# Rolling the columns of a matrix: unaligned long pieces and direct wrapped ends in place of a staged head

## The chip, the cores and the metric

The kernel runs on one core of a Trainium2 chip. The metric is the device time of the program in microseconds, the median of several runs. A core has 16 DMA engines, which move all data here, and several instruction engines which issue the DMAs: SP and ACT, each with a hardware queue (a ring) of its own, and POOL with a software queue. HBM is the chip's main memory, in which the input and output lie; SBUF is the core's on-chip memory of 128 partitions.

## The reference

The whole computation is a rotation of every row by 100 columns.

```python
def setup_inputs():
    return {
        "x": np.random.randn(8192, 8192).astype(np.float32),
        "shift": 100,
    }

def reference(x, shift):
    return np.roll(x, shift, axis=1)
```

A row has 8192 floats, or 32,768 bytes. Output columns 100 to 8191 are input columns 0 to 8091 of the same row, and output columns 0 to 99 (400 bytes, the wrapped end) are input columns 8092 to 8191. No value is changed, so the kernel is a copy of 268.44 MB whose pieces lie 400 bytes further on in the output than in the input.

## The kernel before

With `s = 100` the kernel sets `a = 256`: `s` is rounded up to a multiple of 128 columns, and one more 128 is added where that stays small. The output is cut at column 256, which is byte 1024 of a row.

The body, columns 256 to 8191, goes from HBM to HBM by the loop that ends at L43. The rows are taken in 128 blocks of 64. In the view `(c e j) w -> c j e w` the block is `c`, `e` is one of 16 and `j` one of 4, so that the DMA for one `j` has 16 rows, each four rows from the next, and each of the 16 DMA engines gets one row piece of 31,744 bytes. Even `j` are issued on SP and odd `j` on ACT. In the last 4 blocks each row is cut in two halves, so there are 264 DMAs per queue. A DMA on SP or ACT waits, by the semaphores that the framework gives out, for the fourth DMA before it on its own queue: four are in flight per queue.

The head, columns 0 to 255, goes through SBUF on POOL's queue. It consists of the wrapped end (columns 0 to 99) and of columns 100 to 255. The rows are split into four groups `k` of 2048, each with 128 partitions, `J = 4` and `Q = 4`. For three of every four rows (`q` from 1) a contiguous run of 256 floats is read that starts 100 columns before the row (L73), so it holds the end of the row before and the beginning of this row. The wrapped end of the fourth row and the beginning of the first are read by themselves (L74, L77), and two VectorE copies (L75, L78) put the pieces of each row together in the tile `h`. Then 16 DMAs write `h` to the output, 1024 bytes per row (L82). Nothing else waits for this work, and the body does not wait for it.

Of the kernel before, what the change touches and what calls it, by code (L numbers as in the profile page):

```python
# [1 line left out]

# [4 lines left out]


@with_exitstack
def kernel(  # L10
    ctx: ExitStack,
    tc: tile.TileContext,
    x: bass.AP,
    shift: int,
    out: bass.AP,
):
    nc = tc.nc
    n_rows, n_cols = x.shape
    s = shift % n_cols
    a = -(-s // 128) * 128  # L20
    if 0 < a <= 384 and a + 128 <= n_cols:
        a += 128
    g = a - s
    P = nc.NUM_PARTITIONS
    engines = [nc.sync, nc.scalar]
    n_chunks = 16
    rows = n_rows // n_chunks

    xm = x.rearrange("(c e j) w -> c j e w", e=16, j=4)
    om = out.rearrange("(c e j) w -> c j e w", e=16, j=4)
    if a < n_cols:
        blocks = n_rows // 64
        mid = (a + n_cols) // 256 * 128
        for c in range(blocks):
            parts = ((a, mid), (mid, n_cols)) if c >= blocks - 4 and a < mid else ((a, n_cols),)  # L40
            for j in range(4):
                for lo, hi in parts:
                    engines[j % 2].dma_start(out=om[c, j, :, lo:hi], in_=xm[c, j, :, lo - s:hi - s])  # L43
    if a == 0:
        return


    if a > 512:
        for i in range(n_chunks):
            r = slice(i * rows, (i + 1) * rows)  # L50
            nc.gpsimd.dma_start(out=out[r, :s], in_=x[r, n_cols - s:])
            if g > 0:
                nc.gpsimd.dma_start(out=out[r, s:a], in_=x[r, :g])
        return

    Q, J = 4, 4  # L60
    n_st = n_rows // (P * Q * J)
    reads = ctx.enter_context(tc.tile_pool(name="reads", bufs=n_st))
    heads = ctx.enter_context(tc.tile_pool(name="heads", bufs=n_st))
    xt = x.rearrange("(k p j q) c -> k q p j c", q=Q, j=J, p=P)
    ot = out.rearrange("(k p j q) c -> k q p j c", q=Q, j=J, p=P)
    tiles = []
    for k in range(n_st):
        t = reads.tile([P, Q - 1, J, a], x.dtype)
        h = heads.tile([P, Q, J, a], x.dtype)
        for q in range(1, Q):  # L70
            lead = bass.AP(tensor=x.tensor, offset=(k * P * J * Q + q) * n_cols - s,
                           ap=[[J * Q * n_cols, P], [Q * n_cols, J], [1, a]])
            nc.gpsimd.dma_start(out=t[:, q - 1], in_=lead)  # L73
        nc.gpsimd.dma_start(out=h[:, Q - 1, :, :s], in_=xt[k, Q - 1, :, :, n_cols - s:])  # L74
        nc.vector.tensor_copy(h[:, :Q - 1, :, :s], t[:, :, :, :s])  # L75
        if g > 0:
            nc.gpsimd.dma_start(out=h[:, 0, :, s:], in_=xt[k, 0, :, :, :g])  # L77
            nc.vector.tensor_copy(h[:, 1:, :, s:], t[:, :, :, s:])  # L78
        tiles.append(h)
    for k, h in enumerate(tiles):  # L80
        for q in range(Q):
            nc.gpsimd.dma_start(out=ot[k, q, :, :, :a], in_=h[:, q])  # L82


# [1 line left out]
_INS = ['x', 'shift']  # L86
_OUTS = [((8192, 8192), 'float32')]

_NUMBERS = {'shift': 100}


# [26 lines left out]
```

## Time and profile before

| What | Before |
|---|---|
| Median time, 3 runs | 829.27 us (829.12 to 830.45) |
| Span of the profiled execution | 817.9 us |
| VectorE busy | 7.7 us |
| POOL busy | 28.9 us |
| Body DMAs: SP and ACT, 248 each of 496 KB, 16 each of 248 KB | 12.7 us and under 6 us from issue to landing |
| Head writes: 16 of 512 KB | 112.6 us from issue to landing |

In a profile page, a slice is a fortieth of the span. The row "DMA" gives the mean busy share of the 16 DMA engines in tenths, and "GB/s" what they moved, each byte counted once per DMA. A queue's line gives its packets, its bytes in MB and the time that its packets took, as a share of 16 engines' span. q1 and q10 are the two hardware rings; q0 is POOL's. The HBM line adds up what was read from HBM and what was written to it, so a byte copied from HBM to HBM counts in both. In a table of stages, each line is a stretch of the span with the engines' busy times, the clock, the DMA share and the GB/s.

### The profile page before, as it was taken

Reading aid. Unit: us, or ns where it says so; the run is one execution under the profiler, and the core shown is the slowest. Engines: PE = TensorE matmul, PEld = TensorE weight load, DVE = VectorE, ACT = ScalarE, POOL = GpSimd, SP = SyncE. Lnnn points to the kernel's source line nnn. Section 1 sums busy time; section 2 is a strip of 40 time slices with the busy share of each in tenths; the row PEclk is TensorE's granted clock in tenths of the full one; section 3 lists DMA queues with packets and bytes.
Section 4 is the critical chain, followed back from the end, with each engine's and each line's share of the span. In section 5 each row is a group of like instructions: output and inputs, shape, how many; then the busy total and the mean of one; then the engine's idle time right before and its main releaser. Section 6 shows DMA issues by size and latency. Waiting matters only on the chain. (4 is left out here: it accounts for less than half of the span.)

```text
span 817.9 us, 633 instructions
## 1 busy us (share of the span) xinstructions
DVE 7.7 (1%) x8; POOL 28.9 (4%) x40
## 2 busy tenths in 40 slices
DVE  0000000000000000000000000000000000000000
POOL 3000000010010000000000000000000000000000
DMA  9999999999999999999999999999999999999998
GB/s 307 333 348 342 347 355 347 355 356 344 350 338 363 359 351 354 361 346 360 334 333 341 326 335 331 331 332 337 328 338 331 330 336 331 335 334 326 331 308 299
DMA packets 21572, 276.89 MB, mean 339 GB/s; under 512 B 9024, under 2 KB 9024, under 8 KB 13120
## 3 DMA queue, kind: packets, MB, share of 16 engines
q10 hardware_dynamic: 8448, 130.04, 46.5%
q1 hardware_dynamic: 8448, 130.04, 45.9%
q0 software_dynamic: 4672, 16.78, 6.9%
q14 instruction: 4, 0.03, 0.0%
HBM read 268.44 MB, written 268.44 MB: 656 GB/s over the span
## 5 line engine op out<-in xcount | busy, mean ns | idle before, releaser
L82 POOL DMA_DIRECT2D out_dram<-h x16 | 13.2, 827 | 196.6 <-DMA out_dram<-h 112.1
L73 POOL DMA_DIRECT2D t<-in_x_dram x12 | 9.5, 795 | 60.4 <-DMA h<-in_x_dram 30.1
L75 DVE COPY h<-t 128x1200 f32<-128x1200 f32 x4 | 3.1, 785 | 233.6 <-DMA t<-in_x_dram 233.6
L78 DVE COPY h<-t 128x1872 f32<-128x1872 f32 x4 | 4.9, 1224 | 0.0
L74 POOL DMA_DIRECT2D h<-in_x_dram x4 | 3.0, 749 | 45.6 <-DMA t<-in_x_dram 45.6
L77 POOL DMA_DIRECT2D h<-in_x_dram x4 | 3.0, 751 | 42.8 <-DMA t<-in_x_dram 42.8
L99 POOL MEMSET const-float32-0.0<- 128x1 f32 x1 | 0.1, 100 | 0.2 <-issue 0.2
L99 POOL MEMSET const-bfloat16-1.0<- 128x1 bf16 x1 | 0.1, 103 | 0.0
L99 POOL MEMSET const-float32-1.0<- 128x1 f32 x1 | 0.1, 100 | 0.0
L99 POOL MEMSET const-uint8-127<- 128x1 uint8 x1 | 0.1, 100 | 0.0
## 6 DMA issues: line engine op xcount, KB each, us to landing
out_dram<-in_x_dram ACTq DMA_DIRECT2D x248, 496.0 KB, 12.7
out_dram<-in_x_dram SPq DMA_DIRECT2D x248, 496.0 KB, 12.7
out_dram<-h POOLq DMA_DIRECT2D x16, 512.0 KB, 112.6
t<-in_x_dram POOLq DMA_DIRECT2D x12, 512.0 KB, 95.4
out_dram<-in_x_dram SPq DMA_DIRECT2D x16, 248.0 KB, 5.7
out_dram<-in_x_dram ACTq DMA_DIRECT2D x16, 248.0 KB, 5.9
h<-in_x_dram POOLq DMA_DIRECT2D x4, 312.0 KB, 92.0
h<-in_x_dram POOLq DMA_DIRECT2D x4, 200.0 KB, 97.9
```

The lines of the kernel that those rows point to most:

```text
L73: nc.gpsimd.dma_start(out=t[:, q - 1], in_=lead)
L74: nc.gpsimd.dma_start(out=h[:, Q - 1, :, :s], in_=xt[k, Q - 1, :, :, n_cols - s:])
L75: nc.vector.tensor_copy(h[:, :Q - 1, :, :s], t[:, :, :, :s])
L77: nc.gpsimd.dma_start(out=h[:, 0, :, s:], in_=xt[k, 0, :, :, :g])
L78: nc.vector.tensor_copy(h[:, 1:, :, s:], t[:, :, :, s:])
L82: nc.gpsimd.dma_start(out=ot[k, q, :, :, :a], in_=h[:, q])
L99: nc = _bacc.Bacc("TRN2", target_bir_lowering=False, num_devices=1)
```

## The change

The change drops the cut at column 256, the whole trip through SBUF, POOL's queue and the VectorE copies. Everything goes from HBM to HBM on the two rings.

- The long piece of a row now starts at output column 100. It is 8092 columns, or 32,368 bytes, read from the beginning of the input row and written at byte 400 of the output row.
- A DMA has 32 rows: in the view `(c e h t) w -> c t e h w` each of the 16 engines gets two rows (`h`) which lie two rows apart. SP has `t = 0`, ACT has `t = 1`. The rows of a block thus stand in the same order on each ring as before. There are 128 such DMAs per queue, and no rows are halved at the end.
- The wrapped ends of a block's 64 rows, 400 bytes each, are one DMA, four pieces per engine, issued on ACT and SP in turn. There are 64 such DMAs per queue.

Its purpose is to move each byte by one DMA only, without staging.

```diff
     s = shift % n_cols
-    a = -(-s // 128) * 128
-    if 0 < a <= 384 and a + 128 <= n_cols:
-        a += 128
...
     engines = [nc.sync, nc.scalar]
...
-    xm = x.rearrange("(c e j) w -> c j e w", e=16, j=4)
-    om = out.rearrange("(c e j) w -> c j e w", e=16, j=4)
-    if a < n_cols:
-        blocks = n_rows // 64
-        mid = (a + n_cols) // 256 * 128
-        for c in range(blocks):
-            parts = ((a, mid), (mid, n_cols)) if c >= blocks - 4 and a < mid else ((a, n_cols),)
-            for j in range(4):
-                for lo, hi in parts:
-                    engines[j % 2].dma_start(out=om[c, j, :, lo:hi], in_=xm[c, j, :, lo - s:hi - s])
...
-        for q in range(1, Q):
-            lead = bass.AP(tensor=x.tensor, offset=(k * P * J * Q + q) * n_cols - s,
-                           ap=[[J * Q * n_cols, P], [Q * n_cols, J], [1, a]])
-            nc.gpsimd.dma_start(out=t[:, q - 1], in_=lead)
-        nc.gpsimd.dma_start(out=h[:, Q - 1, :, :s], in_=xt[k, Q - 1, :, :, n_cols - s:])
-        nc.vector.tensor_copy(h[:, :Q - 1, :, :s], t[:, :, :, :s])
...
-    for k, h in enumerate(tiles):
-        for q in range(Q):
-            nc.gpsimd.dma_start(out=ot[k, q, :, :, :a], in_=h[:, q])
+    xb = x.rearrange("(c e h t) w -> c t e h w", e=16, h=2, t=2)
+    ob = out.rearrange("(c e h t) w -> c t e h w", e=16, h=2, t=2)
+    xw = x.rearrange("(c e j) w -> c e j w", e=16, j=4)
+    ow = out.rearrange("(c e j) w -> c e j w", e=16, j=4)
+    for c in range(n_rows // 64):
+        for t in range(2):
+            engines[t].dma_start(out=ob[c, t, :, :, s:], in_=xb[c, t, :, :, :n_cols - s])
+        if s > 0:
+            engines[1 - c % 2].dma_start(out=ow[c, :, :, :s], in_=xw[c, :, :, n_cols - s:])
```

## The prediction

> **What bounds the kernel now.** I read the page first: slices, packets, queues and the HBM line.
>
> ```profile
> DMA  9999999999999999999999999999999999999998
> GB/s 307 333 348 342 347 355 347 355 356 344 350 338 363 359 351 354 361 346 360 334 333 341 326 335 331 331 332 337 328 338 331 330 336 331 335 334 326 331 308 299
> DMA packets 21572, 276.89 MB, mean 339 GB/s; under 512 B 9024, under 2 KB 9024, under 8 KB 13120
> ...
> q10 hardware_dynamic: 8448, 130.04, 46.5%
> q1 hardware_dynamic: 8448, 130.04, 45.9%
> q0 software_dynamic: 4672, 16.78, 6.9%
> ...
> HBM read 268.44 MB, written 268.44 MB: 656 GB/s over the span
> ```
>
> The queue shares add to 99.3%: the 16 DMA engines have a packet in hand almost all the time. That does not yet say that the engines are the limit, since a packet waiting for memory also counts as busy. The slices show about 350 GB/s while the POOL queue runs (slices 3 to 20) and about 332 after it, so I asked for stages.
>
> ```profile
> core 0: us, DVE busy (x) POOL busy (x), PEclk, DMA share, GB/s
> ...
> 180.00:345.00 165.00, 3.28 (x4) 11.10 (x13) 1.00 1.00 353
> 345.00:500.00 155.00, 0.00 (x0) 2.14 (x3) 1.00 1.00 339
> ```
>
> and, of the stages where only the two rings work, and of the edges:
>
> ```profile
> 780.00:800.00 20.00, 0.00 (x0) 0.00 (x0) 1.00 0.89 299
> 800.00:817.90 17.90, 0.00 (x0) 0.00 (x0) 1.00 0.84 297
> ...
> 0.00:4.00 4.00, 0.00 (x0) 2.91 (x8) 1.00 0.44 135
> ...
> 540.00:780.00 240.00, 0.00 (x0) 0.00 (x0) 1.00 1.00 333
> ```
>
> A byte on a ring crosses HBM twice (read and write), one on the POOL queue once, because its other end is SBUF. From 540 to 780 us HBM moves 2 x 333 = 666 GB/s. Cutting the packet records of the trace into 20 us steps and counting ring bytes twice and POOL bytes once gives 645 to 662 GB/s from 40 to 240 us and 650 to 676 after. The sum over HBM stays put while the DMA rate changes, so the bound is HBM traffic.
>
> The packet records agree. A row piece of 31,744 B takes 1.174 us at best (27.0 GB/s; 2,121 of 7,936 are under 1.2 us), but 1.467 us in the mean and about 1.515 in the ring-only stage. While POOL packets keep 2 to 3 of the 16 engines, the other 13 to 14 run at 22 to 24 GB/s each; alone, 16 run at 20.7. Fewer engines on the rings run faster each: they share something, and have slack.
>
> **What the Trainium skill says.** "HBM Reference", Specifications (TRN2), gives about 716 GB/s per domain; the 666 here is 93% of it, so the trace agrees that HBM is near. "DMA: Bandwidth & Descriptors", Issuing engines are not separate DMA queues: all issuers share the same 16 engines; the shares that add to 99.3% agree. The same page, Specifications: under 512 B a DMA does a read-modify-write. The trace has no HBM write under 1,024 B, so no run here shows it; its 400 B reads into SBUF are no slower at best (4,400 B in 171 ns, 25.7 GB/s). The same page, How a descriptor splits into AXI transactions: transactions start at 256 B boundaries, so an unaligned start costs a partial first one. The body now reads from byte 624 of a row, which is unaligned, and still reaches 27.0 GB/s. The section is illustrated by reads; writes are not seen here.
>
> **The change, part by part.** HBM traffic: before, each byte of x is read once and each of out written once. After, the same: 536.87 MB. What leaves is the SBUF trip of columns 0 to 255, so DMA bytes fall from 276.89 to 268.44 MB (3%), q0 with its 6.9% of engine time (0.069 x 817.9 = 56 us per engine) ends, and DVE (7.7 us) and POOL (28.9 us) fall idle. Under an HBM bound these were hidden beside the rings and are worth nothing of themselves.
>
> Body: the ring's pieces grow from 31,744 to 32,368 B, 8,192 of them, at the ring-only rate. Whole output at that rate: 268.44 MB / 333 GB/s = 806.1 us. This includes the bytes of the wraps.
>
> Start: 4 us at 135 in place of 333 GB/s loses 4 x (1 - 135/333) = 2.4 us. It stays.
>
> End: before loses 20 x 34/333 + 17.9 x 36/333 = 4.0 us. It coincides with the half-row pieces of the last 4 blocks: a queue's DMA waits for the fourth before it on that queue, so with half pieces half as much is in flight, and the share falls to 0.89 and 0.84. After, rows stay whole, but an engine gets two rows per DMA, so the last engine may end a row or two (1.5 us each) late. I take 3 us (2 to 5).
>
> Waits: in the built program each DMA of SP or ACT still waits for the fourth before it on its queue. Behind a waiting one stand only that queue's later DMAs, and the DMA engines wait for them once they have drained. Of three DMAs one is a wrap, so four in flight hold at least two long ones: 2 x 2 = 4 rows per engine and ring, where now there are 4 x 1. When the oldest waits for its slowest engine, the others still have up to 4 rows rather than 3. I cost it at nothing; the rows in flight hide it. Issue: 192 instructions per queue, now 264 at 0.51 us (135 us of 818). Even at 1 us each, 192 us, they would lie beside the transfers.
>
> Wraps: 8,192 pieces of 400 B, 512 per engine, in 128 groups of four. Lower bound, by the nearest row (4,096 B packets, 0.158 us at best, four pieces each): 128 x 0.158 = 20 us of engine time. Upper bound, by the slow tail of the 4,000 B packets made of 400 B pieces (0.99 us at the 95th percentile): 128 x 0.99 = 127 us. Slack to hide it: 512 rows x (1.515 - 1.174) = 175 us per engine. As bytes the wraps are already counted; for broken memory words at the seam I add two extra 64 B reads per row (my assumption), 8,192 x 128 B = 1.05 MB / 666 GB/s = 1.6 us, and round it down to 1 with the smaller number of completions. So the small value is taken on the path, and the large one opens the range.
>
> Sum: 806.1 + 2.4 + 3 + 1 = 812.5 us of span, against 817.9. The timed median is 829.27 - 817.9 = 11.4 us above the span; kept, it gives 823.9, say 824.
>
> **Rivals.**
> Wraps on the path: an HBM-to-HBM piece of 400 B may hold its engine. At 0.99 us a group, 127 us or 16% of engine time is in small packets, much as in the POOL stages, where HBM ran near 655 instead of 666: 1.7% of 806, or +14, gives 838. At 2 us a group, 256 us, the rows' 512 x 1.174 x 1.02 = 613 us no longer fit beside them: 869 of span, 880 in time. The read-modify-write note speaks for it; the undisturbed 400 B reads and the 175 us slack speak against. I put it at 838, from 829 to 872.
>
> Unaligned writes broken all along the row: column 100 is byte 400, 16 bytes past a 64 B word. If every write of 256 B broke two words rather than only a row's first and last, HBM would read another 128 B per 256 B: 536.87 + 134 = 671 MB, 1,007 us of span, 1,020 or so. For: the trace shows only aligned HBM writes. Against: the unaligned reads of today show no extra traffic; had they needed 64 B more per 256 B, the stage would move 666 x 1.125 = 749 GB/s, over the stated 716.
>
> Engines as the bound: then dropped engine time is a gain. 512 rows x 1.467 x 32,368/31,744 = 766, wraps 20, completions 128 x 3 x 9 ns = 3.5, edges 5.4: 795 of span, 806 in time. Against it stands that ring packets slow to 1.515 us when the POOL packets go.
>
> **How the numbers follow.** HBM bound with cheap wraps 0.52 (816 to 830; 0.46 faster, 0.05 same, 0.01 slower); wraps on the path 0.26 (0.04 same, 0.22 slower); broken writes 0.14, slower; engines the bound 0.08, faster. So faster 0.54, same 0.09, slower 0.37. The likeliest gives 824. The range from 807 to 872 leaves out the broken writes (0.14) and about half of the engine case.
>
> **What would show it.** Right: HBM line near 660 GB/s over the span, slices level near 333 GB/s with no step at 400 us, long packets at a mean near 1.54 us with a floor near 1.20, wrap packets well under 0.25 us for four pieces, no half-row dip at the end. Wrong: the floor of the long packets above 1.20 us or their mean above 1.6 at equal bytes (broken writes); wrap packets of 0.5 us and more, or a DMA share below 0.97 in mid-span (wraps or waits on the path); slices above 340 (engines had been the bound).

## The result and the profile after

The changed kernel takes 839.06 us (837.30 to 843.37, 6 runs) against 829.35 us for the kernel before on the same chip: a ratio of 1.0114, with a 95% interval of 1.0089 to 1.0138. A repetition gave 1.0132 (1.0111 to 1.0152). The forecast was 824 us and "faster". It is slower by 1.1 to 1.3%.

One thing must be put right before the profiles are compared. The chips differ by about 1%: the kernel before has a median of 819.7 us on one chip of the runs below, and of 827.9 to 828.4 us on the three others. The profile of before that the prediction read has a span of 817.9 us. In every run whose span and time are both known, the time is 1.7 to 2.2 us above the span. That profile thus shows an execution of about 820 us, not one of 829, most likely one on a quicker chip. So all comparisons below are ratios to the kernel before on the same chip, and profiles are set beside others of like speed.

The page of the profile after has these lines of DMA: slices, packets, queues, HBM.

```profile
DMA  9999999999999999999999999999999999999996
GB/s 300 323 331 328 317 338 318 327 325 321 324 322 326 308 326 317 328 323 319 323 316 324 317 322 323 316 310 324 321 326 310 325 319 320 317 328 319 331 331 218
DMA packets 22530, 268.48 MB, mean 319 GB/s; under 512 B 14336, under 2 KB 14336, under 8 KB 14336
q1 hardware_dynamic: 11264, 134.23, 50.1%
q10 hardware_dynamic: 11264, 134.23, 48.4%
HBM read 268.44 MB, written 268.44 MB: 638 GB/s over the span
```

The POOL queue is gone, HBM moves the same 536.87 MB, and the step at 400 us is gone, all as foreseen. But the level rate is about 320 GB/s and not 333, and the last slice falls to 218. The stages of the same run, with the same columns as before:

```profile
core 0: us, POOL busy (x), PEclk, DMA share, GB/s
0.00:4.00 4.00, 0.20 (x4) 1.00 0.51 170
...
540.00:780.00 240.00, 0.00 (x0) 1.00 0.99 320
...
820.00:841.40 21.40, 0.00 (x0) 1.00 0.66 224
```

In the ring-only stage HBM now moves 2 x 320 = 640 GB/s, and in the last 21 us a third of the engines' time is empty, that is, no packet is in hand. The packet records show that the wraps are not slow themselves: a 400 B packet takes 22 to 24 ns at the median and 29 ns in the mean, 0.12 us for a group of four. The long packets have their floor at 1.199 us, which is the floor of before scaled to their length (1.174 x 1.02 = 1.197). Their mean is 1.584 us, where 1.54 was foreseen. So neither kind of packet is slow in its own engine at its quickest; what has fallen is the rate that the engines reach together.

### The profile page after: what moved, and what is told of

The parts are those of the page before. It is cut to its first block, busy times and chain, and to the rows that moved or that the text cites. A ratio compares the mean times of both kernels' runs of the same rounds, so it can differ in the third digit from the quotient of the medians.

```text
span 841.4 us, 429 instructions
## 1 busy us (share of the span) xinstructions
POOL 0.2 (0%) x4
## 3 DMA queue, kind: packets, MB, share of 16 engines
HBM read 268.44 MB, written 268.44 MB: 638 GB/s over the span
```

## Experiments

**The same two kernels on equally quick chips.** First the kernel before, unchanged.

> The kernel before, unchanged, profiled on the same chip as the next three. In the profile of the change the time is 2.0 us above the span (843.37 against 841.4), where the prediction put 11.4 us. If the 11.4 us belong to the kernel before (its POOL queue), the span here is again about 818 with a time near 829. If they are only a profile taken of a quicker execution, the span here is the time less 2 us, about 827, and the HBM sum of the ring-only stage is then below 666 GB/s.

It took 828.52 us (1.0004, 0.9992 to 1.0017), with a span of 827.2 us. Its queues and stages:

```profile
q1 hardware_dynamic: 8448, 130.04, 46.3%
q10 hardware_dynamic: 8448, 130.04, 46.3%
q0 software_dynamic: 4672, 16.78, 6.9%
```

```profile
20.00:400.00 380.00, 7.70 (x8) 22.59 (x28) 1.00 1.00 346
400.00:780.00 380.00, 0.00 (x0) 0.00 (x0) 1.00 1.00 329
```

So on a chip where this kernel takes 828 us, its ring-only stage runs at 329 GB/s, not 333, and the 11.4 us above the span do not exist. The two errors cancelled in the sum: 268.44 MB / 329 is 816 us plus 2, where the prediction had 806 plus 11.4. They are not what turned the sign.

The changed kernel was repeated where before took 828.08 us.

> The changed kernel, unchanged, profiled on the same chip as the next three. Time near 838, span 2 us less, about 320 to 322 GB/s in the middle, and an end of about 10 us in which 4 to 8 engines still work.

It took 838.99 us, with a span of 834.4 us in the profiled execution. The queue lines of its page, and its stages:

```profile
q1 hardware_dynamic: 11264, 134.23, 49.9%
q10 hardware_dynamic: 11264, 134.23, 48.7%
```

```profile
0.00:10.00 10.00, 0.20 (x4) 1.00 0.84 300
20.00:780.00 760.00, 0.00 (x0) 1.00 0.99 324
804.40:834.40 30.00, 0.00 (x0) 1.00 0.78 266
```

The shares give an account of engine time. Here they add to 98.6%, with 12.2 us of the span empty by the packet records; in the kernel before they add to 99.5%, with 4.7 us empty. Packets fill 822.2 us here and 822.5 us there. So dropping 56 us of POOL packets per engine left the filled time where it was, and 7.5 us of emptiness were added: the changed kernel has 3.8 us of it in mid-span and 5.7 us in the last 30 us, where before has none and 3.2. These are single executions; the changed one is 2.5 us quicker than the median of its kernel. The rest of the study asks what refilled the 822 us, and where the emptiness comes from.

**Long pieces without wraps.** Two twins write 8064 columns per row and no wrapped end.

```diff
-            engines[t].dma_start(out=ob[c, t, :, :, s:], in_=xb[c, t, :, :, :n_cols - s])
-        if s > 0:
-            engines[1 - c % 2].dma_start(out=ow[c, :, :, :s], in_=xw[c, :, :, n_cols - s:])
+            engines[t].dma_start(out=ob[c, t, :, :, 100:8164], in_=xb[c, t, :, :, 0:8064])     # unaligned
+            engines[t].dma_start(out=ob[c, t, :, :, 128:8192], in_=xb[c, t, :, :, 28:8092])    # aligned
```

> Left out: the wrapped ends and the last 28 columns; 8064 columns per row are written from column 100 (source column 0), two rows per engine and DMA as in the change. 264.24 MB, which at the 320.5 GB/s of the changed kernel's steady stretch takes 824.5 us, plus about 7 us for start, end and launch: 832. Theory A (the unaligned writes slow HBM): 828 to 834, and slower by 15 us or more than the aligned twin. Theory B (the 400 B wraps slow HBM, or break up the long pieces): the rate returns to about 333 GB/s and the time to about 802, like the twin.

> Left out: output columns 0 to 127. The same 8064 columns per row, but written from column 128 (byte 512) and read from column 28 (byte 112): write aligned, read not. Theory A: long packets at the floor and mean of the kernel before, 333 GB/s, 793 + 9 = 802 us. Theory B: the same time as the unaligned twin, 802. Theory C (two rows per DMA slow the steady rate, nothing else): both near 830.

The ratios are 0.9824 (0.9793 to 0.9855) and 0.9805 (0.9781 to 0.9830): 814.64 and 812.78 us. Both twins run their level stages at 327 to 329 GB/s, close to before's ring-only stage; both have this same line:

```profile
400.00:780.00 380.00, 0.00 (x0) 1.00 1.00 328
```

A row that is written from an unaligned start is therefore not broken all along: the rival of 1,020 us is refuted, and so is any large price on the long pieces. From the unaligned twin to the changed kernel lie, by the ratios (1.0114 and 1.0132), 24 to 26 us for 4.19 MB, which by bytes would be 13. The wraps, or what they meet, cost 11 to 13 us above their bytes.

**What makes a wrap dear.** Three kernels change the size of the wrap, in the changed kernel's layout. Two of them do a rotation by another amount (`roll128`, `roll200`), and the third writes four columns less.

```diff
-            engines[t].dma_start(out=ob[c, t, :, :, s:], in_=xb[c, t, :, :, :n_cols - s])
+            engines[t].dma_start(out=ob[c, t, :, :, 128:], in_=xb[c, t, :, :, :n_cols - 128])  # or 200
-            engines[1 - c % 2].dma_start(out=ow[c, :, :, :s], in_=xw[c, :, :, n_cols - s:])
+            engines[1 - c % 2].dma_start(out=ow[c, :, :, :128], in_=xw[c, :, :, n_cols - 128:])  # or 200
+            engines[1 - c % 2].dma_start(out=ow[c, :, :, :96], in_=xw[c, :, :, n_cols - 100:n_cols - 4])  # ends96
```

> Other work: a rotation by 128 columns. The same bytes and the same DMAs, but long pieces of 32,256 B written at byte 512 and wraps of 512 B, all starts aligned. Theory S (8,192 wraps under 512 B, or words broken at the seam, make HBM read again): both causes are gone, and the steady rate returns to the 328 GB/s of the long pieces alone: 814 us plus 4.2 MB / 328 GB/s x ... as bytes, 12.8, so 826 to 828. Theory P (the price is per piece, a fixed cost of each of the 8,192 small packets): the wraps still cost about as much over their bytes, 836 to 839.

> Other work: a rotation by 200 columns. Wraps of 800 B, over 512 B, but neither 800 nor its half is a multiple of 64 B, so words at the seam stay broken. If wraps under 512 B are dear because they are under 512 B: 826 to 829. If broken words at the seam cost: as the changed kernel, 837 to 840. Theory P (per piece): also 837 to 840, since the pieces are as many.

> Left out: output columns 96 to 99. Wraps of 384 B, a multiple of 64, so that wraps break no word; the long pieces still start in the middle of one, as in the changed kernel. If the wraps' own partial words cost: 829 to 833. If it is their size under 512 B, or their number: 838, less 0.1 MB of bytes (0.4 us).

The rotation by 128 took 0.9950 of before (0.9938 to 0.9962), the one by 200 took 0.9980 (0.9966 to 0.9993), and the wraps of 384 B took 1.0035 (1.0023 to 1.0047), all beside the repeated changed kernel at 1.0132. So a fixed price per piece falls: all have 8,192 wraps, and two of them beat the kernel before. Cutting the wrap from 400 to 384 B saved 0.97%, 8 us, with 0.05% fewer bytes. The rotation by 200 was meant to keep broken words of 64 B above a size of 512 B, and it was cheap; but 800 B is a multiple of 32, so two readings were left, a limit at 512 B and a word of 32 B. The next three kernels part them.

> Other work: a rotation by 104 columns. Wraps of 416 B, a multiple of 32 but not of 64, still under 512; long pieces start at byte 416. Theory T32 (what costs is a broken word of 32 B): the price of the changed kernel goes, 824 to 830. Theory T64 (a broken word of 64 B): 836 to 839 as the changed kernel. Theory N (under 512 B as such costs): as the run with wraps of 384 B, about 830, and not lower.

> Other work: a rotation by 196 columns. Wraps of 784 B, over 512 B, that break a word of 32 B in its middle as the 400 B wraps do; the run with 800 B did not. If the broken word costs whatever the size of the piece: 835 to 839. If it costs only in pieces under 512 B: as the rotation by 200 columns, 825 to 828.

> Left out: output columns 100 to 103. Wraps of 400 B as in the changed kernel, but the long pieces are written from column 104 (byte 416), so the word that the wrap breaks is written by nothing else, and the long piece breaks none of 32 B. If the wrap's broken word costs by itself: 836 to 839. If the price is that two pieces write into one word: 828 to 831, as with wraps of 384 B.

The edits are those above with 104 and with 196. The third keeps the wraps of 400 B and leaves out output columns 100 to 103, so that nothing else writes the word in which a wrap ends:

```diff
-            engines[t].dma_start(out=ob[c, t, :, :, s:], in_=xb[c, t, :, :, :n_cols - s])
+            engines[t].dma_start(out=ob[c, t, :, :, 104:], in_=xb[c, t, :, :, 4:n_cols - s])
```

| Kernel | Wrap | Long piece starts at | Write that breaks a 32 B word | Ratio to before |
|---|---|---|---|---|
| changed, repeated | 400 B | byte 400 | wrap and long piece | 1.0132 (1.0111 to 1.0152) |
| roll196 | 784 B | byte 784 | wrap and long piece | 1.0136 (1.0115 to 1.0157) |
| gap104 | 400 B | byte 416 | wrap | 1.0063 (1.0042 to 1.0085) |
| ends96 | 384 B | byte 400 | long piece | 1.0035 (1.0023 to 1.0047) |
| roll104 | 416 B | byte 416 | none | 0.9973 (0.9963 to 0.9982) |
| roll200 | 800 B | byte 800 | none | 0.9980 (0.9966 to 0.9993) |
| roll128 | 512 B | byte 512 | none | 0.9950 (0.9938 to 0.9962) |

The table orders itself by its fourth column. The chip does not explain this: the changed kernel with half rows at the end, below, has 1.0143 on the chip of the rotations by 104 and by 196. Nor can the reads be the cause, though they break words of 32 B too, in the four dear kernels alone: two edges a row in the first two, but three in `gap104` and `ends96`, which are the cheaper ones. And the aligned twin, which breaks both edges of every read and none of a write, had 0.9805, where a twin that breaks neither has 0.9796 (`long_104`, below).

The stages of the rotation by 104 and of the one by 196, on one chip, show the price as a rate:

```profile
20.00:780.00 760.00, 0.00 (x0) 1.00 1.00 332
786.10:816.10 30.00, 0.00 (x0) 1.00 0.74 255
```

```profile
20.00:780.00 760.00, 0.00 (x0) 1.00 0.99 327
797.90:827.90 30.00, 0.00 (x0) 1.00 0.76 258
```

The kernel with the larger wraps, above 512 B, is the slower one. The Trainium skill's "DMA: Bandwidth & Descriptors", Specifications, puts the limit for read-modify-write at 512 B. For these writes into HBM the runs show no such limit in the time: the rotation with wraps of 416 B is no slower than before, and the one with 784 B pays. What decides is whether the piece's edge lies on a multiple of 32 B. Multiples of 64 B matter little: roll104 breaks such words and stands 0.2% above roll128. Every edge that pays here lies 16 B past a multiple of 32; other offsets were not tried.

In sizes, on 828 us: the wrap's broken word alone costs 1.0063 - 0.9973 = 0.90% (7.5 us), the long piece's alone 1.0035 - 0.9973 = 0.62% (5.1 us), both together 1.59% (13.2 us, with about 2 us of uncertainty). So gap104 lies between its two forecasts because each edge pays its own part. They add up, within their intervals, so it does not need two pieces that meet in one word. Per broken word that is 13.2 us / 16,384 = 0.8 ns, or some 530 B of HBM traffic at the 658 GB/s of roll104. A read-modify-write, as that section has it for small pieces, would fit, but it is not shown: one more read of 64 B would be an eighth of that price, and the profile counts the same reads for roll104 as for the changed kernel, so an extra read is either not there or not counted:

```profile
HBM read 268.44 MB, written 268.44 MB: 658 GB/s over the span
```

Only the price, and what it depends on, is shown.

**The long pieces' share, without wraps.** Was the first pair of twins too coarse to see it?

> Left out: the wrapped ends, and 128 columns of each row in all. 8064 columns per row, two rows per engine and DMA, written from byte 416 to byte 32,672: both ends are multiples of 32, neither of 64 (416), the source starts at column 0. If the long pieces' own broken words of 32 B have a price, this beats the twin from column 100, by 0.3 to 0.8%; if not, they are equal.

> Left out as in the run from column 104; written from byte 400 to byte 32,656, so both ends of every piece break a word of 32 B (16,384 in all). The first look had it 0.2% above a twin with aligned writes, with an interval of 0.4%. If 8,192 broken words of long pieces cost about 5 us (as wraps of 384 B against wraps of 416 B suggest), this is 5 to 10 us above the twin from column 104; if only pieces of a few hundred bytes pay, within 2 us of it.

On one chip the twin from column 104 takes 0.9796 (0.9774 to 0.9819) and the one from column 100 takes 0.9860 (0.9840 to 0.9880): 811.46 against 816.61 us. The price is real, 5.2 us, but here each piece breaks a word at both ends, 16,384 in all. That is 2.6 us for 8,192, half of the 5.1 us found beside wraps. The intervals of about 0.2% on each ratio hardly cover this gap, and the same access pattern had 0.9824 in its first run. If in a long piece only a broken start costs and a broken end does not, 8,192 starts cost 5.2 us here and 5.1 us beside the wraps, and there is no gap. No kernel parts start and end, so this stays open.

**Two rows per DMA, and the end.** One version of the changed kernel takes one row per DMA, and another takes over the half rows at the end.

```diff
-        for t in range(2):
-            engines[t].dma_start(out=ob[c, t, :, :, s:], in_=xb[c, t, :, :, :n_cols - s])
+        for h in range(2):
+            for t in range(2):
+                engines[t].dma_start(out=ob[c, t, :, h, s:], in_=xb[c, t, :, h, :n_cols - s])
```

> The changed kernel with one row per engine and DMA (16 rows, so 256 long DMAs per queue), wraps as they are. Theory C (the two-row DMAs cost): the end, where 4 engines work alone for 6 us in the changed kernel, shrinks, and the time falls by 4 to 5 us to about 834; if the pairing also slows the middle, to about 820. Theories A and B: the middle stays at 640 GB/s over HBM and only the end moves; a ring that holds four DMAs of which one or two are wraps then has as little as 2 rows in flight, which may cost up to 10 us.

> The changed kernel with the end of the kernel before: in the last 4 blocks one row per engine and DMA, each row in two halves. All else as changed. The theory that the two-row DMAs cost at the end alone: the 10 us in which a part of the engines works alone shrink to about 3 us, and the time falls by 3 to 5 us to 834 or 835. If the 6 us that the one-row version gained lie in the middle: no change, 837 to 839.

One row per DMA took 1.0056 (1.0044 to 1.0068), so it gains 0.6 to 0.8% on the changed kernel (1.0114 and 1.0132). The half rows in the last 4 blocks gained nothing: 1.0143 (1.0120 to 1.0167). I had thought that the two-row DMAs cost at the end alone; the runs refute the cure, and the stages of the half-row kernel show why:

```profile
780.00:790.00 10.00, 0.00 (x0) 1.00 1.00 314
790.00:800.00 10.00, 0.00 (x0) 1.00 0.70 244
800.00:820.00 20.00, 0.00 (x0) 1.00 0.92 316
820.00:826.70 6.70, 0.00 (x0) 1.00 0.55 180
```

Half rows make what is in flight smaller at 790 us. In the next 10 us 30% of the engine time is empty, and the last 7 us are poor as well. The reading that fits is that engines drift apart by as many rows as are in flight: when that number shrinks, or when the work ends, those ahead wait. This drift was not followed engine by engine. The loss was moved, not removed. In the one-row kernel fewer rows are in flight all along:

```profile
q1 hardware_dynamic: 13312, 134.24, 49.9%
q10 hardware_dynamic: 13312, 134.24, 49.2%
```

```profile
20.00:780.00 760.00, 0.00 (x0) 1.00 1.00 325
799.70:829.70 30.00, 0.00 (x0) 1.00 0.86 287
```

Its last 30 us keep 0.86 of the engine time full, against 0.78 in the repeated changed kernel. By the packet records its packets fill 822.2 us, exactly as there; 7.6 us are empty, against 12.2. So what one row per DMA saves is emptiness: 2.5 us in mid-span and 2.0 at the end.

Is it so without wraps?

> Left out as in the run from column 100, and its pieces, with one row per engine and DMA. The theory that two rows in a DMA cost at the end only, because more rows are in flight and the engines drift further apart: 3 us less than the two-row run. If two-row DMAs also slow the middle: 5 to 7 us less, as with the wraps. If the gain came from the wraps standing between shorter DMAs: no difference.

No: 0.9862 (0.9841 to 0.9883) against 0.9860 for two rows. The end does get shorter, 4.2 us empty in its last 30 against 7.5, but packets fill 806.5 us instead of 803.9. The gain of one-row DMAs thus shows only with wraps in the rings. A ring holds four DMAs, and in the changed kernel one in three is a wrap that carries 25 KB, in the one-row kernel one in five; that this starves an engine now and then would fit its mid-span emptiness, but was not tried. The twins without wraps have 1.8 and 2.9 us of emptiness in mid-span as well, so wraps can't be all of it.

**What the staged head was worth.** The kernel before without its head:

```diff
-    Q, J = 4, 4
...
-    for k, h in enumerate(tiles):
-        for q in range(Q):
-            nc.gpsimd.dma_start(out=ot[k, q, :, :, :a], in_=h[:, q])
```

> Left out: the head, output columns 0 to 255, with all of POOL's and VectorE's work; the rest as in the kernel before. 7936 of 8192 columns: by bytes the ratio is 0.969. If the staged head costs no more than its bytes in HBM: 0.968 to 0.971. If the 56 us of engine time of its packets are only partly hidden: 0.955 to 0.965.

It took 798.11 us, 0.9639 (0.9622 to 0.9657). The head costs 30.3 us of 828.4. By the bytes that it writes it would be 1/32 of the time, 25.9 us. So all that could be saved on the head is about 4.4 us, though its packets hold 56 us of every engine. That is the second of the two ranges expected, in which the engine time is not hidden in full, but most of it was. This supports the bound that the prediction chose, and the rival with the engines as the bound (806 us) falls.

The queue has another side. Without POOL the body leaves 3.8 us of engine time empty before its last 60 us and after the start, by the packet records; with POOL there is no emptiness there. 2.9 us of the 3.8 lie between 20 and 400 us, the stretch in which before has POOL's packets (its line, 1.00 and 346, is shown above):

```profile
20.00:400.00 380.00, 0.00 (x0) 1.00 0.99 327
```

So POOL's packets seem to fill gaps that the two rings leave; these are single executions.

**Versions without broken words for the real rotation.** Both have one row per DMA from column 104. One puts columns 0 to 103 together in SBUF, by POOL's DMAs without VectorE; the other sends columns 0 to 95 from HBM to HBM and only columns 96 to 103, 32 B per row, through SBUF. The cut shows the first against the one-row version.

```diff
-                engines[t].dma_start(out=ob[c, t, :, h, s:], in_=xb[c, t, :, h, :n_cols - s])
+                engines[t].dma_start(out=ob[c, t, :, h, 104:], in_=xb[c, t, :, h, 4:n_cols - s])
...
+        nc.gpsimd.dma_start(out=m[:, :, :s], in_=xt[k, :, :, n_cols - s:])     # head104
+        nc.gpsimd.dma_start(out=m[:, :, s:], in_=xt[k, :, :, :4])
...
+        nc.gpsimd.dma_start(out=ot[k, :, :, :104], in_=m[:, :, :])
```

> The whole rotation by 100. Long pieces one row per engine and DMA from column 104 (a multiple of 32 B), the head of 104 columns put together in SBUF by POOL's DMAs alone (400 B and 16 B reads, 416 B writes, no VectorE). No HBM write breaks a word of 32 B. From the rotation by 104 (0.997 of before) less the gain of one-row DMAs (0.006): 0.99, if its 24,576 small packets are hidden; if each costs its time on the path (28 us per engine in all, of which the direct wraps already had 12), 1.01.

> The whole rotation by 100, with only the broken word through SBUF: wraps of 384 B from HBM to HBM, long pieces one row per engine and DMA from column 104, and columns 96 to 103 (32 B per row, read as 16 B and 16 B) put together in SBUF by POOL's DMAs. If a small packet costs about 10 ns of its engine and HBM does not mind: 0.99 to 1.00. If writes of 32 B alone in a 64 B word are dear: 1.005 to 1.02, above the run that stages 104 columns.

They took 1.0008 (0.9994 to 1.0022) and 1.0002 (0.9991 to 1.0014): both as quick as the kernel before, neither quicker, and both 1% below the changed kernel. They are also 0.5% below the one-row version with its broken words (1.0056), although they add small packets; so on the real rotation at least a part of the price goes with the broken words. The gain that the rotation by 104 plus one-row DMAs seemed to promise (0.99) was not reached. The 416 B head keeps 8.6 us of emptiness and the 32 B one 10.7, so part of it went there; the rest of their cost was not taken apart. No version in this study beats the kernel before on the real rotation.

## Why the prediction was wrong

The sign was wrong, and one term of the sum, the broken words that it priced under "Wraps", made it so.

- **The bound** (HBM traffic, near 660 GB/s, so the POOL queue's 56 us of engine time are hidden): right. Removing the head alone saves 4.4 us over its bytes. On a chip where before takes 828 us the level is 2 x 329 GB/s.
- **Body at the ring-only rate, 806.1 us, and 11.4 us above the span**: both wrong, because the profile was taken on a quicker execution than the times, and they cancelled (816 + 2). The error is setting a profile's span and another run's time side by side as if they were one; that the sum held all the same is luck.
- **Wraps, 1 us**: the step that turned the sign. Their engine time was small, as stated: 0.12 us for a group of four, below even the lower bound of 0.158. But the broken words, put in by assumption at two reads of 64 B a row and rounded to 1 us, cost 13.2 us. Their price was eight times the assumed 1.6 us: what failed is pricing a broken word by the bytes of two more reads. No row of the profile of before could show it, since both its HBM writes start and end on multiples of 512 B; the bound on the unknown should have been wider on this term, and the range (up to 872) did hold the time of 839.
- **End, 3 us, and waits at nothing**: too small. Counted as emptiness, before has 4.7 us in all and the changed kernel 12.2. By the reading above, which is not shown, the four rows in flight that were to hide the waits also let the engines drift apart, and at the end those ahead stand idle; some 3.8 us are empty in mid-span, where POOL's packets seem to have filled gaps. The prediction had 3 us at the end in place of 4 and nothing in mid-span; 7.5 us were added.
- **Removal, the gain**: real, but small. With no broken word (rotation by 104) the changed layout takes 0.9973 of before, emptiness included. That is a gain of 2.2 us, less than half of the 5.4 us forecast. Beside the prediction's profile of before, an execution of like speed (817.9 against 816.1 us), its packets fill 803.2 us in place of 811.9, but 12.8 us are empty in place of 6.0: of 8.7 us gained, emptiness takes 6.8 back. It shrank the gain; only the broken words turned it into a loss.

With the measured terms, on a chip of 828.1 us: 828.1 - 2.2 (the layout without broken words) + 7.5 (wraps' broken words) + 5.1 (those of the long pieces) = 838.5, and 838.99 was measured.

**The rivals.** "Wraps on the path" named 838 us, and 839 came, but by another way: the wrap's packets do not hold their engine, and the slack did hide them. Its number was right by chance. "Writes broken all along the row" is refuted by the long pieces without wraps, though a small relative of it, words broken at the edges of the pieces, is the cause. "Engines as the bound" is refuted by the body alone.

## What to carry to other kernels

Let pieces that are written to HBM start and end on multiples of 32 B, also the small ones; a price of 0.8 ns per broken edge is nothing for a few and 13 us for 16,384. A busy share near 100% on the DMA engines can be memory at its limit; then taking engine time away gains little (here 4.4 us for 56). More rows in flight went with a longer end (the last 30 us keep 0.78 of the engine time full with two rows per DMA, 0.86 with one), which need not change the time, as the twins without wraps show. A profile and a table of times belong together only if the time is the span plus a known small rest.

## What the runs showed of the hardware

Before the runs I had expected a limit at 512 B or a word of 64 B; it is a word of 32 B, for a piece of 784 B as much as for one of 400 B, as far as edges 16 B past a multiple of 32 tell. A small HBM-to-HBM packet costs little in its engine: 24 ns at the median for 416 B, 27 ns for 512 B, 38 ns for 800 B. And smoothing the end with half rows moved a part of the loss some 30 us ahead of the end without making it smaller.
